# Two attention layers on one core: gate products moved to the end of the second attention, context shift rows on another queue, one modulation one tile later

## The chip, the core and the metric

The kernel runs on one core of a Trainium2 chip. The metric is the device time of one execution in microseconds (us). The core has TensorE for matrix products (PE in the profile, with its weight loads as PEld), VectorE (DVE), ScalarE (ACT), GpSimd (POOL) and SyncE (SP), which here only issues transfers. Each engine works through its own instruction stream in order; an instruction that must wait for another engine or for a transfer holds up all that stands behind it on its engine.

## What is computed

Two layers over 1024 latent tokens and 256 context tokens of width 1024, all in float32. Each layer modulates a normed input, runs attention, gates the result and adds it to the stream:

```python
shift, scale, gate = adaln_params(c, w_mod, b_mod)          # silu(cond) @ w_mod + b_mod, split in 3
shift_c, scale_c, gate_c = adaln_params(c_ctx, w_mod, b_mod)
h = rms_norm(x, norm_w) * (1.0 + scale[:, None, :]) + shift[:, None, :]
hc = rms_norm(ctx, norm_w) * (1.0 + scale_c) + shift_c
y, yc = mixer(h, hc, mixer_params, cos, sin, with_ctx_out)  # attention * silu(g), times w_out
x = x + gate[:, None, :] * y
```

Layer 0 is grouped-query attention (16 query heads, 4 key heads, 64 wide); latent tokens read context and latent keys, context tokens read context alone. Layer 1 is multi-head latent attention: keys and values come from a 256-wide compressed row through `w_kv_b`, queries from a 384-wide one. Layer 1 returns only the latent stream, so its context tokens give keys and values but no output, and only the gate of `c` (not of `c_ctx`) is needed there.

## The kernel before

**Stages, in order of time.** (1) Layer 0's modulation and projections up to about 300 us, by a hand-written plan. (2) Layer 0's attention, about 330 to 704 us. (3) Layer 0's output projection, 704 to 825 us, which also norms, modulates and transposes the tokens for layer 1. (4) The keys and values of layer 1 ("kv stage"), 825 to about 925 us. (5) Layer 1's queries and gate path, to 1140 us. (6) Layer 1's attention, 1140 to 1544 us. (7) Layer 1's output projection to the end.

**Precision.** Most matrix products are made in three parts (high times high, high times low, low times high) of values that are split in two: ACT casts the high half, DVE or POOL subtracts it (`split`, `load_weight`, `modulate`). Weights come through a ring of three raw buffers of [128, 1024] float32 (`rawp`, tag `wraw`), are cast on ACT (line 184) and subtracted on DVE or POOL (line 163).

**Attention.** `Attention.run` goes through units, one head of latent queries each (1024 queries, ten key tiles of 128) and, in layer 0, four more for the context queries of a key group (two key tiles). For each key tile TensorE makes five (layer 0: four) score products per half, ACT takes the exponential into `p` (line 607), and beside them TensorE makes the maxima of later units, which DVE reduces out of PSUM (lines 454, 465, 495, 497). After the last key tile `do_av` multiplies by the values (line 654). POOL adds the `p` tiles of a unit up (line 640). The order on PE, DVE, ACT and POOL is that of the program (`manual_schedule`); SP's order, and that of most other stages, is laid out by a scheduler when the kernel is built.

The row maxima are folded into the scores as an extra row, the shift row: `do_shift` turns the maxima on DVE (line 95, into `turned`) and copies two rows with a transfer into the unit's operand (`crow`): line 521, issued by ACT while `run` is under way. The turns run at one point of each unit, between its scores and its `do_av` (line 805); in the same place stand the sums of the unit before (`total_by_squares`), the transposing reductions of this unit (line 99, `squares`) and, on every second unit while some are left, the casts of an output weight piece (lines 818 to 821).

**Layer 1's gate.** Its gate vector is a product of `l1_w_mod` (transposed, rows 2048 to 3071) with a row `u`. `mod_cols` makes it as eight DVE instructions of 128x1024 with a sum (line 265), `mod_cols_end(2)` adds the bias, turns the result and stores it to `gated[1]`; it is read at the start of stage 7 (`load_x`, line 864). The eight stand in the kv stage, one per token tile, in the `later_with_cols` step of `staged`; each loads 512 KB into a `wraw` buffer. DVE's order in the kv stage is the program's (`in_order`), so each of them stands between the latent split of one tile and the key norm of another.

**Layer 0's output projection.** Each of ten token tiles takes 48 products (lines 120 to 122); `add` multiplies by the gate row, adds the old x (buffer `xt`, four of them), and `sink0` stores it to `x1d`, norms it in place (lines 305, 144, 146, 307) and gathers tiles in pairs. `modulate` transposes a pair on TensorE (line 319, 16 transposes), scales and shifts it on DVE (line 323) and splits it on ACT and DVE/POOL. `sink0` calls `flush(1)` at tiles 2, 4, 6 and 8, so that pair 0 (tiles 0 and 1) is modulated behind tile 2, pair 1 behind tile 4, and so on. The first two tiles are finished together, since the projection starts on partial sums.

## Time and profile before

| | |
|---|---|
| median of 3 runs | 1639.27 us (1636.88 to 1641.38) |
| profiled execution, its own time | 1638.23 us |
| its span, first to last instruction | 1636.3 us |
| mean granted TensorE clock | 0.995 |
| TensorE busy of the span | 98% |
| DVE, POOL, ACT busy | 70%, 59%, 39% |
| HBM moved | 171.23 MB read, 73.63 MB written |

The profile is one execution. "Busy" is the time in which an engine had an instruction; a wait is the idle time before an instruction, put down to what released it. In rows of a timeline the first number is the start in us from the first instruction, the second the duration in us; a row can stand for several like instructions ("x15"), and the idle time before it, with its releaser, is in brackets at the end. Rows of a wait view give the total in us, the number of times and the longest. "PEq", "ACTq" and "SPq" mark the sequencer of an engine, which issues transfers. Line numbers (L265) are those of the kernel before.

### The profile page before, as it was taken

To read this page: it belongs to the slowest core of one execution; us is meant where nothing else is said; L and a number is where in the kernel's file an instruction comes from. 1 tells how busy PE (TensorE), PEld (TensorE's weight loads), DVE (VectorE), ACT (ScalarE), POOL (GpSimd) and SP (SyncE) were. 2 spreads that over 40 slices of the span, in tenths; PEclk is the share of its full clock that TensorE was granted. 3 is DMA by queue.
4 is the path that set the end of the run, shared out by engine and by line. 5 is a ranking of instruction groups with operands and counts; after the bars stand their busy time and mean duration, and the time that the engine had idled before them with its cause. 6 is when DMAs were issued, how large, how long until landed. Compare 5 with 4: busy or idle time off the path is not lost.

```text
span 1636.3 us, 26486 instructions
## 1 busy us (share of the span) xinstructions
PE 1596.0 (98%) x9788; PEld 1178.3 (72%) x9788; DVE 1150.5 (70%) x1951; ACT 641.2 (39%) x943; POOL 961.7 (59%) x629
## 2 busy tenths in 40 slices
PE   7999999999999999999989999999999999999998
PEld 5776788865554555577878798987776767767587
DVE  2674876679998988746576767755778888788231
ACT  3652321235654555522244543341444544435310
POOL 2673640138999999923245555450768878777521
PEclk9999999999999999999999999999999999999999
DMA  8636566742533342274246867768456565562451
GB/s 285 213 106 192 170 196 231 215 134 56 130 82 98 94 108 78 71 224 152 96 138 182 239 200 201 221 202 197 114 137 154 124 149 117 136 145 70 131 179 64
DMA packets 215325, 246.77 MB, mean 151 GB/s; under 512 B 19802, under 2 KB 157266, under 8 KB 215196
## 3 DMA queue, kind: packets, MB, share of 16 engines
q1 hardware_dynamic: 214228, 244.83, 53.7%
q8 instruction: 77, 1.26, 0.3%
q14 instruction: 52, 0.43, 0.1%
q10 hardware_dynamic: 968, 0.25, 0.1%
HBM read 171.23 MB, written 73.63 MB: 150 GB/s over the span
## 4 chain that ended last, share of the span: by engine, by line
PE 84%; DMA 5%; DVE 4%; POOL 2%; ACT 2%; issue 2%; SPq 1%; DVEq 0%; POOLq 0%; ACTq 0%
PE st L600 21%; PE avt L654 9%; PE av L654 9%; PE mm L120 8%; PE mm L122 8%; PE mm L121 8%; PE mx L452 4%; PE y L120 3%; PE y L121 3%; PE y L122 3%; PE mx L486 2%; DVE wb L163 1%; DMA q1l<-tl 1%; PE mx L462 1%; DMA mraw<-in_l_w_mod 1%
## 5 line engine op out<-in xcount | busy, mean ns | idle before, releaser
L640 POOL TENSOR_TENSOR acp<-acp,p 128x1024 f32<-128x1024 f32 x188 | 448.6, 2386 | 12.6
L607 ACT ACTIVATE p<-st 128x1024 f32<-128x1024 f32 x328 | 336.3, 1027 | 154.5 <-PE st L600 145.7
L454 DVE TENSOR_REDUCE m<-mx 128x1 f32<-128x512 f32 x256 | 175.8, 691 | 66.2 <-PE mx L452 60.3
L640 POOL TENSOR_TENSOR acp<-p 128x1024 f32<-128x1024 f32 x34 | 81.5, 2398 | 191.7 <-ACT p L607 191.7
L495 DVE TENSOR_REDUCE m<-mx 128x1 f32<-128x1024 f32 x128 | 150.2, 1219 | 39.4 <-PE mx L486 38.9
L654 PE MATMUL avt<-p,v 128*64 128x512 f32 x672 | 149.3, 596 | 0.7 <-ACT p L607 0.6
L654 PE MATMUL av<-p,v 128*64 128x512 f32 x640 | 141.1, 595 | 0.0
L163 POOL TENSOR_TENSOR wb<-wraw,wa 128x512 fp32r<-128x512 f32 (+3 forms) x65 | 91.0, 1415 | 80.4 <-ACT wa L184 80.4
L120 PE MATMUL mm<-wa,hh 128*128 128x512 f32 (+2 forms) x336 | 126.1, 375 | 1.7 <-ACT hh L1041 1.1
L600 PE MATMUL st<-QH,KH 64*128 64x512 f32 x320 | 122.5, 407 | 0.6 <-DVE gth L354 0.5
L122 PE MATMUL mm<-wa,hl 128*128 128x512 f32 (+2 forms) x336 | 121.5, 362 | 1.6 <-DVE hl L1044 1.6
L121 PE MATMUL mm<-wb,hh 128*128 128x512 f32 (+2 forms) x336 | 121.1, 360 | 0.0
L600 PE MATMUL st<-QH,KL 64*128 64x512 f32 x320 | 117.9, 391 | 0.0
L600 PE MATMUL st<-QL,KH 64*128 64x512 f32 x320 | 117.6, 390 | 0.0
L654 PEld LDWEIGHTS avt<-p,v 128*64 128x64 f32 x672 | 46.0, 137 | 93.8 <-issue 82.9
L654 PEld LDWEIGHTS av<-p,v 128*64 128x64 f32 x640 | 44.3, 137 | 87.9 <-issue 87.3
L120 PE MATMUL mm<-hh,wa 128*128 128x512 f32 (+1 forms) x264 | 103.0, 390 | 0.9 <-ACT th L102 0.9
L120 PE MATMUL y<-wa,oh 128*128 128x512 f32 (+1 forms) x268 | 103.3, 386 | 0.0
L122 PE MATMUL y<-wa,ol 128*128 128x512 f32 (+1 forms) x268 | 102.8, 384 | 0.0
L121 PE MATMUL y<-wb,oh 128*128 128x512 f32 (+1 forms) x268 | 102.8, 384 | 0.0
L122 PE MATMUL mm<-hh,wb 128*128 128x512 f32 (+1 forms) x264 | 101.3, 384 | 0.0
L121 PE MATMUL mm<-hl,wa 128*128 128x512 f32 (+1 forms) x264 | 101.3, 384 | 0.0
(267 smaller groups left out, 4045.1 us busy)
## 6 DMA issues: line engine op xcount, KB each, us to landing
wraw<-in_l_w_in SPq DMA_DIRECT2D x28, 512.0 KB
wcols<-in_l_w_mod_t SPq DMA_DIRECT2D x24, 512.0 KB
KH<-k1h SPq DMA_DIRECT2D x32, 320.0 KB
KL<-k1l SPq DMA_DIRECT2D x32, 320.0 KB
rb<-rrow SPq DMA_DIRECT2D x72, 128.0 KB
mraw<-in_l_w_mod SPq DMA_DIRECT2D x16, 512.0 KB
wraw<-in_l_w_out SPq DMA_DIRECT2D x16, 512.0 KB
QA<-q0h SPq DMA_DIRECT2D x32, 256.0 KB
```

Source lines behind the costliest of these rows:

```text
L120: pe.matmul(ps, lhsT=lh(k), rhs=rh(k), start=first and i == 0, stop=False)
L121: pe.matmul(ps, lhsT=lh(k), rhs=rl(k), start=False, stop=False)
L122: pe.matmul(ps, lhsT=ll(k), rhs=rh(k), start=False, stop=last and i == len(ks) - 1)
L163: eng.tensor_sub(lo, a, b)
L452: pe.matmul(held["m"][:, cs], lhsT=q[:, t * P:(t + 1) * P], rhs=k[:, ks], start=j == 0, stop=j == len(pairs) - 1)
L454: dve.reduce_max(s["m"][:, i, n:n + 1], held["m"], axis=AX.X)
L486: pe.matmul(m[:, n * 512:n * 512 + 512], lhsT=q[:, i * P:(i + 1) * P], rhs=k[:, n * 512:n * 512 + 512], start=True, stop=True)
L495: dve.reduce_max(s["m"][:, i, 0:1], m, axis=AX.X)
L600: pe.matmul(ps[:, n * 512:(n + 1) * 512], lhsT=lh, rhs=rh, start=j == 0, stop=j == last)
L607: act.activation(p, ps, AF.Exp, scale=self.ops["scale"])
L640: pool.tensor_add(t, a, b)
L654: pe.matmul(s["av"][64 * n:64 * n + 64, :], lhsT=s["v"][:, kt, u["vc"]:u["vc"] + 64], rhs=p[:, n * 512:(n + 1) * 512], start=kt == kts[0], ...
```

## The change

Three things are edited.

1. The shift rows of context units are issued by SP while `run` is under way; those of latent units stay on ACT.
2. In `sink0`, `flush` is no longer called at tile 2 but at tile 3, before tile 3 joins tile 2 in the list of held pairs. Pair 0 is modulated behind the fourth tile (tile 3), pair 1 behind tile 4 as before.
3. The eight gate products of layer 1 and the load of `u` leave the kv stage. `run` gets a table `beside` of calls by unit and by whether the group is the unit's last; they run just ahead of `do_av`. In layer 1's attention unit 10 loads the first two weight pieces, units 11, 12 and 13 make one product each, unit 14 two, and the first group of unit 15 (the last unit, whose key tiles are cut in six and four) the last three and the end. Each product but the last two loads the piece two further on.

```diff
@@ Attention.__init__
+            self.beside = {}
@@ do_shift, turn
-                    (act if self.running else sp).dma_start(raw(s["crow"][n]), r[4 * n:4 * n + 4, :])
+                    (act if self.running and u["kind"] == "lat" else sp).dma_start(raw(s["crow"][n]), r[4 * n:4 * n + 4, :])
@@ Attention.run
                             self.squares(u, p2s[n1 // 2:])
+                        self.beside.get((t, int(end)), lambda: None)()
                         if t % 2 and end:
@@ sink0
-            if tt % 2 == 0:
+            if tt % 2 == 0 and tt != 2 or tt == 3:
                 flush(1)
-            else:
+            if tt % 2:
                 hold.append((tt // 2, xs_of[tt // 2]))
@@ kv stage
-        u = st.enter_context(tc.tile_pool(name="urow1", bufs=1, **right)).tile([P, D], F32, name="u0", tag="u0")
-        sp.dma_start(u, ud[0:1, :].broadcast_to([P, D]))
-
-        def gate_cols(k):
-            w = rawp.tile([P, D], F32, name="wcols", tag="wraw")
-            sp.dma_start(w, ins["l1_w_mod_t"][2 * D + k * P:2 * D + (k + 1) * P, :])
-            mod_cols(w, u.unsqueeze(1), w, 2, k, (0,))
-            if k == KT - 1:
-                mod_cols_end(2)
...
-            staged(range(TT), kv_compress, kv_latent, later_with_cols, later, kv_expand, store_all_but_last)
+            staged(range(TT), kv_compress, kv_latent, later, later, kv_expand, store_all_but_last)
@@ ahead of layer 1's at.run
+    u = stE.enter_context(tc.tile_pool(name="urow1", bufs=1, **right)).tile([P, D], F32, name="u0", tag="u0")
+    sp.dma_start(u, ud[0:1, :].broadcast_to([P, D]))
+    cols = {}
+
+    def gate_fetch(k):
+        cols[k] = rawp.tile([P, D], F32, name="wcols", tag="wraw")
+        sp.dma_start(cols[k], ins["l1_w_mod_t"][2 * D + k * P:2 * D + (k + 1) * P, :])
+
+    def gate_cols(n):
+        for _ in range(n):
+            k = cols.pop("next", 0)
+            mod_cols(cols[k], u.unsqueeze(1), cols[k], 2, k, (0,))
+            cols["next"] = k + 1
+            if k + 2 < KT:
+                gate_fetch(k + 2)
+            if k == KT - 1:
+                mod_cols_end(2)
+
+    at.beside = {(10, 1): lambda: [gate_fetch(k) for k in range(2)], (11, 1): lambda: gate_cols(1), (12, 1): lambda: gate_cols(1),
+                 (13, 1): lambda: gate_cols(1), (14, 1): lambda: gate_cols(2), (15, 0): lambda: gate_cols(3)}
     at.run(24, 2, pieces, lambda: first.extend(fetch_first(1, 3)))
```

## The prediction

> **What bounds the kernel now.** The page's first section comes first:

> ```profile
> span 1636.3 us, 26486 instructions
> PE 1596.0 (98%) x9788; PEld 1178.3 (72%) x9788; DVE 1150.5 (70%) x1951; ACT 641.2 (39%) x943; POOL 961.7 (59%) x629
> ```

> TensorE lacks 40.3 us of the span. The change takes no product from it, so it can win only where TensorE stands still or runs at a lower clock. So I read the waits of PE next (us in total, times, longest):

> ```profile
> PE mmk L120 <- DVE kn L1714: 2.3, 2, 1.5
> PE tp L319 <- DVE xt L307: 2.2, 1, 2.2
> PE tp L1955 <- DVE tl L103: 2.0, 1, 2.0
> PE mx L486 <- DVE m L495: 1.9, 2, 1.4
> ...
> PE st L600 <- ACT os L675: 1.1, 1, 1.1
> ...
> PE mmv L120 <- ACT v L1736: 1.0, 1, 1.0
> ...
> PE mmv L120 <- ACT sq L1729: 0.8, 1, 0.8
> ```

> Each of the three edits has its own waits here: L1714, L1736 and L1729 in the kv stage (mmk, mmv), L319 at pair 0, L486 and L600 in layer 0's attention. I then read the timelines around each.

> **Edit 3, what it removes.** First the steady part of the kv stage, one tile long, by the windows view (length, then busy us of PE, PEld, DVE, ACT, POOL, clock):

> ```profile
> 877.66:887.49 9.83, 9.83 (x61) 8.77 (x60) 6.74 (x17) 4.50 (x13) 5.98 (x8) 1.00 0.70 202
> ```

> PE is busy for all of it, so a shorter DVE gains nothing here. What can go are the waits at the ends. The products, and the stretch in which the last one stands (DVE, then POOL, then ACT):

> ```profile
> L265 DVE SCALAR_TENSOR_TENSOR wcols<-wcols,u x8: 1201/1204/1843, 850.6 to 907.5; 128x1024 f32<-128x1024 f32 x8
> 907.53 1.84 DVE L265 SCALAR_TENSOR_TENSOR wcols<-wcols,u 128x1024 f32<-128x1024 f32 x1
> 909.77 0.15 DVE L271 TENSOR_TENSOR top<-cols,colsT 128x8 f32<-128x8 f32 x1
> 909.96 0.86 DVE L95 STREAM_TRANSPOSE turned<-top 32x32 f32<-32x32 f32 x4
> 910.85 0.69 DVE L1731 TENSOR_REDUCE kss<-sq 128x8 f32<-128x512 f32 x1
> 905.91 2.38 POOL L163 TENSOR_TENSOR wb<-wraw,wa 128x384 fp32r<-128x384 f32 x2
> 910.91 0.51 ACT L184 CAST wa<-wraw 128x384 fp32r<-128x384 f32 x1 [2.30 <-DMA wraw<-in_l_w_in]
> ```

> Ahead of the key sums at 910.85 stand 1.84 + 0.15 + 0.86 = 2.85 us that go. They delay L1714, for which PE waits 2.3 us in two places. ACT waits 2.30 us for a weight piece whose buffer comes from the ring that the products' loads also use; without them it loads sooner, and the copy of v behind it, for which PE waits 1.0 us, too. So the drain's 3.3 us go nearly whole; I take 2.9, since the two POOL roots per tile stay in DVE's chain. At the fill, the 0.8 us at 863.9 stands behind three products (850.65, 854.77, 859.27) and goes. The other waits before 858 come ahead of the first product or from ACT, and stay. Sum: **3.7 us**, bounds 1.0 (only the buffer wait) and 4.1 (all of these waits). The eight loads, the load of u and the store to gated leave SP here too.

> **Edit 3, what it adds.** At the attention's end, one unit's gap and the last unit's rows:

> ```profile
> 1400.00:1500.00 100.00, 100.00 (x742) 69.91 (x742) 81.73 (x135) 42.67 (x44) 75.61 (x36) 1.00 0.51 120
> 1441.19 2.31 DVE L99 TRANSPOSE_TENSOR_REDUCE squares<-p 128x64 f32<-128x2048 f32 x1
> 1445.66 1.39 DVE L454 TENSOR_REDUCE m<-mx 128x1 f32<-128x512 f32 x2 [2.16 <-PE mx L452]
> 1439.03 4.80 POOL L640 TENSOR_TENSOR acp<-acp,p 128x1024 f32<-128x1024 f32 x2
> 1528.86 9.72 POOL L640 TENSOR_TENSOR acp<-acp,p 128x1024 f32<-128x1024 f32 x4
> 1540.35 3.77 DVE L871 TENSOR_TENSOR ol<-oraw,oh 128x896 fp32r<-128x896 f32 x3 [16.54 <-ACT oh L870]
> 1532.04 1.75 SPq L839 DMA_DIRECT2D oraw<-od  x3
> 1541.94 0.64 PE L720 MATMUL mx<-acp,twos 128*32 128x256 f32 x8
> ```

> In units 11 to 13 the product stands where DVE now idles 2.16 us. It needs 1.20 to 1.84 us (the second beside POOL's subtractions), so it fits: 0. In unit 14 no maxima follow that PE waits for. In unit 15 DVE idles 16.54 us and the three products need 3.6 to 5.5, but POOL adds without pause beside them. If each holds an addition back by its own 1.2 us, the last addition ends at 1538.6 + 3.6 = 1542.2 against PE's 1541.94: 0.3 us lost. Bounds 0 and 3.6. I take **0.3**. On SP the three oraw loads now wait for the last products' buffers, and behind them sg, od, gb and xt; with products that end by 1537 the loads come about 4 us later than 1532, while ol starts at 1540 and PE has three tiles to make: 0, and 2 if that cover is gone. The moved 4.7 MB fall on 100 us with a DMA share of 0.51: 0.

> [...]

> **Edit 2, pair 0.** PE, DVE, the chain and two windows:

> ```profile
> 737.34 0.30 PE L319 MATMUL tp<-ident,xt 128*128 128x128 f32 x1 [0.29 <-DVE x_ms L144]
> 739.80 2.81 PE L319 MATMUL tp<-ident,xt 128*128 128x128 f32 x15 [2.16 <-DVE xt L307]
> 738.44 1.30 DVE L307 TENSOR_SCALAR xt<-xt,x_rs 128x1024 f32<-128x1024 f32 x1 [0.58 <-DMA x1d<-xt]
> 735.46 2.88 DMA x1d<-xt
> 737.05:740.50 3.45, 1.00 (x7) 0.84 (x8) 2.82 (x6) 0.85 (x1) 1.82 (x2) 1.00 0.73 213
> 740.50:743.90 3.40, 3.40 (x15) 3.11 (x14) 3.40 (x8) 2.18 (x4) 0.78 (x2) 0.50 0.09 22
> ```

> The norm in place waits for the store of the same tile, and the transposes wait for the norm: 0.29 + 2.16 = 2.45 us idle. Right behind it the clock is 0.50 for 3.40 us, all of them busy: 1.70 us more. One tile later (about 11 us) the tile has been ready since 739.7, so both go: **4.15 us**, bounds 2.45 (the clock drops elsewhere) and 4.15. What is late next: pair 1's second tile has about 12 us from its last product to its transposes, where pair 0's had the same and lost 2.45 with two tiles finished at once; here one is. The loads of x for tiles 4 and 5 need pair 0's buffers and start some 7 us later; with 2.88 us a tile (the store's row) they land before tile 4's addition, 11 us on. SP's stores and oraw loads may queue behind these; I cost that 0, its price is the 2 us of another norm.

> [...]

> **Edit 1, shift rows.** ACT, DVE, then the same place one context unit later, then the tile's own view:

> ```profile
> 495.83 0.58 ACTq L521 DMA_DIRECT2D shift<-turned  x1
> 496.98 2.38 ACTq L521 DMA_DIRECT2D shift_ctx<-turned  x2
> 499.40 1.14 ACT L184 CAST wa<-wraw 128x512 fp32r<-128x512 f32 x2 [8.68 <-DMA sg<-sgd]
> 495.85 2.31 DVE L99 TRANSPOSE_TENSOR_REDUCE squares<-p 128x64 f32<-128x2048 f32 x1
> 500.57 1.86 DVE L163 TENSOR_TENSOR wb<-wraw,wa 128x512 fp32r<-128x512 f32 x1 [2.41 <-ACT wa L184]
> 529.88 0.50 PE L486 MATMUL mx<-KA,QA 64*128 64x512 f32 x2 [0.57 <-DVE m L495]
> L600 PE MATMUL st<-shift_ctx,minus x16: 385/388/394, 431.7 to 699.9; 64*128 64x512 f32 x16
> L521 ACTq DMA_DIRECT2D shift_ctx<-turned x8: 580/580/619, 405.3 to 669.9; - x8
> ```

> Of the four context turns only this one is followed by a wait: 1.1 (os) and 1.4 (m, of the 1.9) = 2.4 us. Without the two issues ACT casts at 496.4 instead of 499.4, DVE subtracts when its reduction ends (495.85 + 2.31 = 498.2) instead of 500.57, and the maxima follow 2.4 us sooner. One unit on, with the casts in time, 0.57 remain, so I take 2.4 - 0.4 = **2.0 us**, bounds 0 (the latent row still waits behind SP, and the casts with it) and 2.4. On SP the row waits for DVE's turn, with QA, QL and rb queued behind; the first use (431.7) is 26 us behind the first issue (405.3), so that is 0, at worst 2.

> **Sum.** 3.7 + 4.15 + 2.0 - 0.3 = 9.55. On the profiled execution: 1638.23 - 9.55 = 1628.7; it lies 1.04 under the median, so for the median 1639.27 - 9.55 = **1629.7 us**.

> **Rivals.**
> A. DVE's and POOL's own chain keeps the kv stage's end: edit 3 wins 1.0 or less, 1632.4, and with its 2 us of tail 1634.1. For it: POOL's roots stay; against: 2.85 us leave the chain at its latest point. 0.15.
> B. Pair 0 behind tile 3 meets another wait of 2 us and the low clock: edit 2 wins nothing, 1633.9. For it: x loads later; against: 11 us of room. 0.10.
> C. More goes than that: the 2.0 us at L1955 lies in a stage whose order the scheduler lays out anew, and weight pieces now load sooner; with 1.7 for a low clock behind it as at pair 0, 3.7 less: 1626.0. 0.12.
> D. Slower: the same new order sets casts and subtractions of weight pieces between the query tiles, so that PE stalls there as at L1955, 3.7 us each. From the third on it outweighs the gain: 1629.7 + 3 x 3.7 = 1640.8, from the fourth 1644.5. For it: one such stall stands there already; against: only one in some 200 us. 0.08.
> E. The edits don't bite: the scheduler leaves the waits in new places, 1638 to 1640. 0.05.

> **How the numbers follow.** The forecast (1627.5 to 1632) has 0.50. About 0.3% (4.9 us) is what a measurement here can tell from no change: 1634.4 and 1644.2. Faster: 0.50 + 0.13 of A + 0.05 of B + 0.12 = 0.80, of which I keep 0.77 for the part of the forecast lost to several small shortfalls. Slower: 0.04 of D and 0.01. Same: the rest, 0.18. The range leaves out D, E and the far end of C: 1625.0 to 1637.5.

> **What would show it.** No PE wait on L307 and a clock of 1.00 around pair 0; no wait on L675 near 501; waits on L1714, L1736 and L1729 under 1 us in sum; the products at 1.2 to 3.6 us in units 11 to 15 with no PE wait on DVE maxima, and under 1 us at L720. It is wrong if PE's idle time falls by less than 5 us, or if new waits appear in the query stage or at layer 1's output projection.

## The result, and the profile after

| | before | changed |
|---|---|---|
| median, 4 runs each on one chip | 1638.30 us (1636.88 to 1641.38) | 1622.22 us (1620.82 to 1623.37) |
| ratio | | 0.9899, 95% interval 0.9883 to 0.9914 |
| profiled execution, its span | 1636.3 us | 1620.2 us |

The change wins 16.1 us, by the interval 14.1 to 19.2. Forecast were 9.55 us, with 1625.0 as the lower end of the range: the direction was right, the size too small. One run of a kernel below (edit 3 alone) took 3203.56 us at a granted clock of 1.00, for a reason that the record does not show; its ratio leaves that run out. The first lines of the page of the changed kernel, and its waits of PE (us in total, times, longest); its line numbers are one or two higher, and in the query stage 13 lower:

```profile
span 1620.2 us, 26475 instructions
PE 1590.2 (98%) x9788; PEld 1182.7 (73%) x9788; DVE 1159.2 (72%) x1951; ACT 641.4 (40%) x943; POOL 961.1 (59%) x629
...
PE tp L1703 <- DVE kvn L1684: 3.7, 3, 1.3
...
PE tp L1942 <- DVE tl L103: 2.3, 2, 2.0
PE mx L487 <- DVE m L496: 1.8, 2, 1.2
PE y L108 <- ACT oh L872: 1.6, 2, 1.0
...
PE mmv L120 <- ACT v L1738: 0.5, 1, 0.5
```

PE's waits on L319, L675 (os) and L1714 are gone from the list, and of the fill's waits on `v` and `sq` nothing is left. But PE's idle time (span less busy) falls only from 40.3 to 30.0 us, 10.3; the other 5.8 us lie in PE's busy time, though it makes the same 9788 products. That PE is busy for fewer microseconds over the same work is the first thing to explain here.

To place the gain, take the same matrix product in both traces (the n-th with the same operands) and subtract its starts. The gain up to a stage's first product and up to its last one differ by what the stage won:

| place | won, us | forecast |
|---|---|---|
| start, to layer 0's attention (code unchanged) | 1.1 | 0 |
| layer 0's attention ahead of the turn, near 466 | -0.3 | 0 |
| turn near 496 (edit 1) | 1.5 | 2.0 |
| pair 0 (edit 2) | 4.5 | 4.15 |
| kv stage (edit 3) | 7.8 | 3.7 |
| query stage | 3.6 | 0 |
| layer 1's attention | -1.2 | 0 |
| its end and the output projection | -1.05 | -0.3 |

The sum, before rounding, is 16.1. Two rows of the table make most of the surplus: the kv stage and the query stage.

### The profile page after: what moved, and what is told of

It reads as the page before. It is cut to its first block, busy times and chain, and to the rows that moved or that the text cites. A ratio compares the mean times of both kernels' runs of the same rounds, so it can differ in the third digit from the quotient of the medians.

```text
span 1620.2 us, 26475 instructions
## 1 busy us (share of the span) xinstructions
PE 1590.2 (98%) x9788; PEld 1182.7 (73%) x9788; DVE 1159.2 (72%) x1951; ACT 641.4 (40%) x943; POOL 961.1 (59%) x629
## 3 DMA queue, kind: packets, MB, share of 16 engines
q8 instruction: 77, 1.26, 0.3%
## 4 chain that ended last, share of the span: by engine, by line
PE 87%; DVE 5%; DMA 3%; POOL 2%; ACT 1%; issue 1%; SPq 0%; DVEq 0%; ACTq 0%; POOLq 0%
PE st L601 19%; PE mm L120 9%; PE avt L655 8%; PE mm L122 8%; PE mm L121 8%; PE av L655 8%; PE mx L453 4%; PE y L121 4%; PE y L122 4%; PE y L120 4%; PE mx L487 2%; PE mx L463 1%; DVE wb L163 1%; DVE wcols L265 1%; DMA mraw<-in_l_w_mod 1%
## 5 line engine op out<-in xcount | busy, mean ns | idle before, releaser
L163 POOL TENSOR_TENSOR wb<-wraw,wa 128x512 fp32r<-128x512 f32 (+3 forms) x65 | 92.0, 1431 | 75.4 <-ACT wa L184 75.4
L120 PE MATMUL mm<-wa,hh 128*128 128x512 f32 (+2 forms) x336 | 125.6, 374 | 1.1 <-ACT hh L1043 1.1
L120 PE MATMUL mm<-hh,wa 128*128 128x512 f32 (+1 forms) x264 | 103.1, 390 | 0.0
L120 PE MATMUL y<-wa,oh 128*128 128x512 f32 (+1 forms) x268 | 102.9, 384 | 0.0
```

Source lines behind the costliest of these rows:

```text
L120: pe.matmul(ps, lhsT=lh(k), rhs=rh(k), start=first and i == 0, stop=False)
L163: eng.tensor_sub(lo, a, b)
```

## The experiments

All times are device times, each against runs of the kernel before on the same chip (medians 1636.99 to 1637.44). "Ledger" is the comparison above, with the first profile of before as the reference, at one place of one profiled execution.

**The three edits, each alone.** Each kernel is the one before with one of the diff's three parts.

> The kernel before with edit 1 alone (context shift rows by SP). Theory A, that each edit's share is what the changed kernel's PE timeline shows at its own place: 1.2 us less than before (the wait for os, 1.08, goes; of the wait for m 1.2 stays, since the DVE subtraction is longer beside POOL), and nothing in the kv and query stages. Theory B, that the surplus over the forecast (about 6 us) comes from the scheduler's new order whichever edit is made: 3 us or more less here, with waits gone in the query stage too.

> The kernel before with edit 2 alone (pair 0 modulated behind tile 3). Theory A: PE's waits at L319 (0.29 and 2.16) go, and so does a clock of 0.50 right behind them where a run of before has it: 2.7 to 4.5 us less. No other stage changes. Theory B: also less in the kv stage, whose first tiles follow 90 us on.

> The kernel before with edit 3 alone (gate products at the attention's end). Theory A: the kv stage wins 7.8 us (3.8 at its first tiles, 4.0 at its last), the query stage 0.9 to 1.9 by waits that go (the one at tl L103 of 2.0 stays; a clock of 0.50 behind it comes or not), the end loses 1.0: in sum 8 to 11 us less. Theory B, as forecast: 3.4 us less from the edit itself, the rest only together with the other edits.

| | median, us | ratio, interval | gain by the ratio |
|---|---|---|---|
| edit 1 | 1636.38 | 0.9997, 0.9988 to 1.0006 | 0.5 (-1.0 to 2.0) |
| edit 2 | 1632.50 | 0.9965, 0.9951 to 0.9978 | 5.7 (3.6 to 8.0) |
| edit 3 | 1630.24 | 0.9951, 0.9937 to 0.9964 | 8.0 (5.9 to 10.3) |

The three sum to 14.2, near the 16.1: the edits add up, and a surplus that comes whichever edit is made (theory B) is not seen. By the ledger edit 1 alone wins 1.7 at its turn, edit 2 alone 4.5 at pair 0 and nothing in the kv stage (5.0 before it, 5.1 behind it), edit 3 alone 7.9 in the kv stage. Edit 1's gain is too small for its timing to tell. It also has a price that nobody forecast: in all six profiles with this edit PE loses 0.26 to 0.30 us near 466, and in none without it; what makes it stays open. So edit 1 wins 1.2 to 1.5 us in sum.

Why edit 1 wins less than 2.4: the timelines at that turn, DVE and POOL with edit 1 alone, then POOL of before (DVE's subtraction there: 500.57, 1.86 us):

```profile
493.74 2.31 DVE L99 TRANSPOSE_TENSOR_REDUCE squares<-p 128x64 f32<-128x2048 f32 x1
495.98 2.68 DVE L163 TENSOR_TENSOR wb<-wraw,wa 128x512 fp32r<-128x512 f32 x1
495.73 2.38 POOL L640 TENSOR_TENSOR acp<-acp,p 128x1024 f32<-128x1024 f32 x1
```

```profile
497.05 4.83 POOL L640 TENSOR_TENSOR acp<-acp,p 128x1024 f32<-128x1024 f32 x2
```

The subtraction follows the reduction at once, as forecast, but lasts 2.68 us (2.81 in the changed kernel) where it had lasted 1.86. In both kernels it ends 0.55 us after the POOL addition that was running when it began: 498.66 after 498.11, and 502.43 after 501.88. It begins earlier and waits longer, so 0.8 to 0.95 us of the gain are given back, and a wait for m of 1.1 to 1.2 stays.

**Is ACT still the bound at that turn?** All shift rows on SP, the latent ones too:

```diff
-                    (act if self.running else sp).dma_start(raw(s["crow"][n]), r[4 * n:4 * n + 4, :])
+                    sp.dma_start(raw(s["crow"][n]), r[4 * n:4 * n + 4, :])
```

> The kernel before with all shift rows issued by SP, latent ones too. If the ACT casts of the weight piece were still the bound at the turn near 496, the wait for m (1.0 to 1.2 us with edit 1 alone) shrinks by up to 1 us. If DVE's own reduction and subtraction are the bound there, as the changed kernel's trace says, nothing is won against edit 1 alone. A loss comes if the latent rows stand behind SP's waits and scores wait for their shift row: then waits at st by st<-shift in every unit, 16 units of 0.5 us or more.

1656.50 us, ratio 1.0113 (1.0097 to 1.0128): 18.5 us slower. PE's waits in layer 0's attention, and SP ahead of the first of them:

```profile
PE st L600 <- DMA shift<-turned: 12.0, 2, 6.2
PE mx L486 <- DVE m L495: 1.6, 2, 1.0
```

```profile
478.69 0.38 SPq L744 DMA_DIRECT2D od<-os  x1
479.11 0.48 SPq L734 DMA_DIRECT2D sg<-sgd  x1
479.64 0.59 SPq L1415 DMA_DIRECT2D QA<-q0h  x1
480.34 1.38 SPq L521 DMA_DIRECT2D shift<-turned  x2
```

The wait for m is as with edit 1 alone (1.6 us in sum in both), so the ACT casts are no longer the bound there. The loss came in two units, not in all sixteen as the expectation had it: a latent row that stands behind SP's od, sg and QA makes PE wait 5.8 and 6.2 us. Each wait brings 6.83 us at a clock of 0.50 with it, so that by the ledger the two cost 8.2 and 8.6 us. That the changed kernel leaves these rows on ACT is what makes edit 1 safe.

**The kv stage: DVE's time, or the ring?** The kernel before with short products (all, then only those with k < 4), and with whole products but no loads:

```diff
-            mod_cols(w, u.unsqueeze(1), w, 2, k, (0,))
+            mod_cols(w[:, :8], u.unsqueeze(1)[:, :, :8], w[:, :8], 2, k, (0,))
```

```diff
-            w = rawp.tile([P, D], F32, name="wcols", tag="wraw")
-            sp.dma_start(w, ins["l1_w_mod_t"][2 * D + k * P:2 * D + (k + 1) * P, :])
-            mod_cols(w, u.unsqueeze(1), w, 2, k, (0,))
+            dve.scalar_tensor_tensor(u, u, 0.5, u, op0=ALU.mult, op1=ALU.add, accum_out=sums_of[2][:, k, 0:1])
```

> The kernel before with the eight gate products of the kv stage made over 8 of 1024 columns; the loads, their ring buffers and SP's stream stay. It leaves out 1016 of 1024 columns of each gate product. Theory A, that DVE's time in the kv stage's chain makes the loss: the kv stage wins 6 to 7.5 us of the 7.8, at its first tiles 3.5 to 3.8. Theory R, that the ring's buffers and loads make it: 2 us or less, all at the end, and the first tiles keep their waits at L1702 (1.37) and on v L1736 (0.68 twice).

> The same, but only the first four products over 8 columns, the last four whole. It leaves out 1016 of 1024 columns of four gate products. Theory A: the kv stage wins the 3.8 us of its first tiles and nothing at its end, where the waits at L1714 (1.47, 0.80) and L1736 (0.99) stay. Rival, that a delay at the first tiles is what reaches the end: 6 us or more.

> The kernel before with the eight products made on the resident row tile, with no loads and no ring buffers; DVE's instructions have the same size. It leaves out the weight matrix of the gate products (another sum is formed). Theory A: the first tiles keep all their waits (3.8 us); at the end ACT's wait for wraw (2.30) goes and of the 4.0 us there at most 1 to 1.5 is won. Theory R: 2 us or more at the end and something at the first tiles.

| | median, ratio | fill, ledger | end, ledger |
|---|---|---|---|
| all short | 1627.37, 0.9947 (0.9932 to 0.9963) | 3.6 | 2.5 |
| first four short | 1630.73, 0.9960 (0.9945 to 0.9975) | 3.6 | 1.0 |
| no loads | 1638.78, 1.0007 (0.9995 to 1.0018) | 0.0 | 0.0 |
| changed kernel | | 3.8 | 4.0 |

(Without loads the fill has the same four waits as before: 1.36, 0.67, 0.68 and 0.76 us. A slot of half clock, of which more below, fell into it in that profile and took 1.4 us; it is left out of the 0.0.) The fill's gain comes with DVE's shorter work alone. At the end each cause hides behind the other: free of the loads alone nothing is won, free of DVE's work alone 2.5, free of both 4.0. (With the first four short, 1.0 was won at the end where the expectation had nothing: the wait for v fell there from 1.0 to 0.2.) With short products the end's wait is this one of ACT, on the load, with the copy of v behind it:

```profile
910.20 0.51 ACT L184 CAST wa<-wraw 128x384 fp32r<-128x384 f32 x1 [3.26 <-DMA wraw<-in_l_w_in]
910.62 0.58 ACT L1736 COPY v<-mmv 128x512 f32<-128x512 f32 x1
```

A rival is left open here. The order of PE's and ACT's instructions in this stage is laid out when the kernel is built, and it is not the same in these kernels. With short products and in every kernel with edit 3, three of PE's transposes in the fill and ten of ACT's instructions stand earlier than before; without loads PE's order is the old one, and so are the fill's waits. So the runs show that DVE's work is the cause, but not how much of the fill's gain comes from waiting less in the same order and how much from the new order. In the query stage, up to 1140 us, PE, DVE and ACT have the same order before and after.

**How a product of 1.20 us makes a wait of 1.37.** The fill of the kernel before, POOL, DVE and PE, then the changed kernel's POOL at the same tile:

```profile
850.23 0.26 POOL L1693 TENSOR_TENSOR krt<-kvn,ropeB 128x32 f32<-128x32 f32 x1
850.56 1.41 POOL L1694 TENSOR_TENSOR kvn<-krt,krt 128x32 f32<-128x32 f32 x1
850.65 1.20 DVE L265 SCALAR_TENSOR_TENSOR wcols<-wcols,u 128x1024 f32<-128x1024 f32 x1
851.79 0.14 DVE L1677 TENSOR_SCALAR kvms<-kvss 128x1 f32<-128x1 f32 x1
852.02 0.28 PE L1702 MATMUL tp<-ident,kvn 128*32 128x128 f32 x1 [1.37 <-POOL kvn L1694]
853.91 0.50 PE L120 MATMUL mmk<-wa,kvh 128*128 128x512 f32 x1 [0.68 <-ACT v L1736]
857.98 0.40 PE L120 MATMUL mm<-wa,hh 128*128 128x288 f32 x1 [0.68 <-ACT v L1736]
```

```profile
843.64 0.25 POOL L1696 TENSOR_TENSOR kvn<-krt,krt 128x32 f32<-128x32 f32 x1
```

POOL's small addition took 1.41 instead of 0.25 us: it ends 0.12 us behind DVE's product. And DVE's next norm (L1677) starts 1.1 us late. To tell the two apart the product is replaced by an instruction that reads one input:

```diff
-            mod_cols(w, u.unsqueeze(1), w, 2, k, (0,))
+            dve.tensor_scalar(w, w, 0.5, 0.0, op0=ALU.mult, op1=ALU.add, accum_out=sums_of[2][:, k, 0:1])
```

> The kernel before with each gate product replaced by a DVE instruction over the same 128x1024 tile that reads one input instead of two. It leaves out the factor u of the gate products. Theory L, that the first wait of the kv stage's fill (1.37 at L1702) comes from POOL being held beside DVE's two-input instruction (its addition L1694 took 1.41 us instead of 0.25): that addition takes 0.25 to 0.4 us and the wait at L1702 falls to some 0.2. Theory C, that DVE's own time is enough: at an unchanged duration of 1.2 us on DVE the wait stays at 1.0 or more. If the instruction itself takes half the time the run says less: then the later waits on v L1736 (0.68 twice) shrink by about as much.

1633.26 us, ratio 0.9978 (0.9967 to 0.9989). The first such instruction, POOL ahead of it, and PE's wait:

```profile
847.68 0.25 POOL L1694 TENSOR_TENSOR kvn<-krt,krt 128x32 f32<-128x32 f32 x1
847.77 1.20 DVE L1767 TENSOR_SCALAR_CACHE_REDUCE wcols<-wcols 128x1024 f32<-128x1024 f32 x1
847.99 0.28 PE L1702 MATMUL tp<-ident,kvn 128*32 128x128 f32 x1 [0.21 <-POOL kvn L1694]
```

DVE works for the same 1.20 us, POOL's addition takes 0.25 us again, and the wait at L1702 falls from 1.37 to 0.21; by the ledger the fill wins 1.3 of its 3.8 us. Theory L holds for that wait. The other 2.5 stay where DVE's own time stays; that they pass through DVE's late norm is argued, not shown.

**The end: SP.** The changed kernel with a table of calls that begins and ends one unit earlier:

```diff
-    at.beside = {(10, 1): lambda: [gate_fetch(k) for k in range(2)], (11, 1): lambda: gate_cols(1), (12, 1): lambda: gate_cols(1),
-                 (13, 1): lambda: gate_cols(1), (14, 1): lambda: gate_cols(2), (15, 0): lambda: gate_cols(3)}
+    at.beside = {(10, 1): lambda: [gate_fetch(0), gate_fetch(1), gate_cols(1)], (11, 1): lambda: gate_cols(1), (12, 1): lambda: gate_cols(1),
+                 (13, 1): lambda: gate_cols(2), (14, 1): lambda: gate_cols(3)}
```

> The changed kernel with the products earlier: one in each of units 10 to 12, two in 13, three in 14, none in 15. Theory A, that the 0.98 us wait at the first product of the output projection comes from SP, where the three oraw loads stand behind the gate store that waits for the last products: that wait goes, 1.0 us less than the changed kernel (about 1621 against 1622). Rival: the second product of unit 13 does not fit DVE's gap of 2.16 us and PE waits there for maxima, some 1 us, so that nothing is won or 0.5 lost.

> The changed kernel with the products in units 10 to 14, again, on the same chip as the changed kernel itself. If the end's wait behind SP's gate store is what it wins: 1.1 to 1.4 us under the changed kernel, sometimes 1.7 more where a slot of half clock would have followed that wait (as in the run of edit 3 alone). If it was a luckier chip: the two agree within 0.5 us.

> The changed kernel, beside the one with the earlier products. The first product of the output projection waits 1.0 to 1.3 us for oh, the 2.0 us at tl L103 stay, and a slot of half clock follows them only if they lie whole between two edges of the raster of 3.413 us.

Earlier products: 1618.63 us (0.9884, 0.9871 to 0.9897), and on another chip 1619.37 (1617.86 to 1620.72; 0.9891, 0.9877 to 0.9906) beside the changed kernel's 1623.22 (1620.91 to 1623.28; 0.9911, 0.9894 to 0.9927). The ranges of the single runs don't overlap there, though the intervals of the ratios do. The medians lie 3.85 us apart there, more than the 1.1 to 1.4 expected. By the ledger of the two profiles, 4.4 us apart, 1.6 lie at the end; 2.6 lie in the query stage, where only the changed kernel's profile has a slot of half clock. SP of the changed kernel (first profile) and the projection's first product, then SP of the earlier products (second run):

```profile
1517.81 0.30 SPq L274 DMA_DIRECT2D gated<-turned  x1
1518.20 0.45 SPq L735 DMA_DIRECT2D sg<-sgd  x1
...
1520.67 2.09 SPq L737 DMA_DIRECT2D rb<-rrow  x2
1522.80 1.80 SPq L841 DMA_DIRECT2D oraw<-od  x3
1528.15 0.50 PE L108 MATMUL y<-wa,oh 128*128 128x512 f32 x1 [0.98 <-ACT oh L872]
```

```profile
1504.62 0.30 SPq L274 DMA_DIRECT2D gated<-turned  x1
...
1512.72 1.75 SPq L841 DMA_DIRECT2D oraw<-od  x3
```

In the changed kernel the loads start 5.0 us behind the gate store, about 8 us later in the program than before (1532.04 less the 17.1 us won by then is 1514.9). The first product of the projection (1528.15) then waits 0.98 us for oh; in the other profiles of the changed kernel 1.26 and 1.53, with edit 3 alone 2.0. With the earlier products no wait of PE is left from 1130 us to the end of layer 1's attention, in both runs. The rival, a wait for maxima in unit 13, did not show.

**The clock.** The changed kernel once more:

> The changed kernel again, for the clock: theory G, that the clock of 0.50 covers one slot of a fixed raster of about 3.41 us and follows a slot in which PE was busy under half, with a phase that differs from execution to execution: the waits of 2.0 us at tl L103 in the query stage is followed by a slot of 0.50 in those executions alone in which it lies whole in one slot (some 4 in 10). Rival: the clock depends on the wait's length alone, and since it did not fall behind this wait in the changed kernel's first profile it does not here. Otherwise as the first profile, 1622.

1620.85 us (0.9899, 0.9883 to 0.9916). The wait of 2.0 us at tl L103 in the query stage is in all fourteen profiles. Windows of the slot in which it begins and of the next one, in before, in the first profile of the changed kernel and in its third (length, busy us of PE, PEld, DVE, ACT, POOL, clock):

```profile
996.54:999.95 3.41, 1.38 (x11) 1.09 (x10) 2.97 (x9) 0.00 (x0) 1.46 (x3) 1.00 0.96 294
999.95:1003.36 3.41, 3.41 (x12) 3.41 (x11) 3.25 (x12) 1.84 (x4) 2.22 (x3) 0.50 1.10 360
```

```profile
979.87:983.28 3.41, 2.74 (x17) 2.38 (x15) 3.15 (x10) 0.49 (x1) 3.24 (x4) 1.00 0.87 224
983.28:986.69 3.41, 2.06 (x13) 2.09 (x14) 3.20 (x9) 0.82 (x2) 0.61 (x2) 1.00 1.11 372
```

```profile
979.95:983.36 3.41, 1.38 (x10) 1.05 (x9) 2.98 (x9) 0.00 (x0) 1.97 (x3) 1.00 0.92 258
983.36:986.77 3.41, 3.41 (x12) 3.41 (x13) 3.34 (x11) 1.72 (x4) 1.71 (x3) 0.50 1.11 366
```

The same wait is followed by half the clock in the first and third and not in the second, where an edge splits it: the raster of theory G holds, and its rival falls with the third profile. Its "busy under half" (1.71 us) is no exact bound: slots with 1.66 us busy (before, at 911.15) and 1.53 (earlier products, first run, at 979.96) were followed by the full clock, slots with 1.73 (edit 2 alone, at 496.44) and 2.14 (all rows on SP, at 1122.63) by half. Within every profile the starts of such slots lie whole multiples of 3.4133 us apart (before: 740.53 and 999.95, 76.0 of them). In five of the fourteen profiles the wait lay whole between two edges, and in these five alone the slot of 0.50 followed; in the other nine an edge cut it, at worst 1.88 on one side.

## Why the prediction came out too low

- **Edit 3, what it removes: the step that failed.** The forecast took 3.7 us, and the stage won 7.8. Two parts of the step were wrong. (a) "The other waits before 858 come ahead of the first product or from ACT, and stay": three of them, 1.37, 0.68 and 0.68 us at 852.02, 853.91 and 857.98, come behind the first product (850.65) or the second (854.77) and go when those are short. POOL's held addition makes the first; the two on v, with ACT as the last link, go with DVE's shorter work, through its late norm or through the order laid out for it. (b) Idle time was taken as the whole price of a wait: the change "can win only where TensorE stands still or runs at a lower clock". The windows of the stage, from the same product to the same product, before, changed, and with one-input instructions:

```profile
828.00:940.00 112.00, 100.84 (x578) 84.92 (x578) 77.20 (x184) 53.21 (x135) 56.28 (x65) 1.00 0.67 197
```

```profile
821.09:925.27 104.18, 98.74 (x578) 85.61 (x578) 66.95 (x163) 54.19 (x136) 52.26 (x65) 1.00 0.58 169
```

```profile
825.12:935.33 110.21, 101.33 (x578) 84.87 (x578) 75.75 (x184) 53.02 (x135) 51.63 (x65) 1.00 0.67 201
```

 All hold the same 578 products, at a clock of 1.00. In the changed kernel the stage is 7.82 us shorter, PE is idle for 5.72 us less, and busy for 2.10 us less. Around one wait it looks like this (kernel before, PE):

```profile
921.59 0.39 PE L122 MATMUL mmv<-wa,kvl 128*128 128x512 f32 x1
922.78 0.50 PE L120 MATMUL mmk<-wa,kvh 128*128 128x512 f32 x1 [0.80 <-DVE kn L1714]
923.11 0.39 PE L121 MATMUL mmk<-wb,kvh 128*128 128x512 f32 x1
923.35 0.40 PE L122 MATMUL mmk<-wa,kvl 128*128 128x512 f32 x1
```

 Such products otherwise start 0.23 us apart, and a row's 0.39 overlaps the next one's. Here the starts are 1.19 and then 0.33 apart: 0.96 + 0.10 = 1.06 us are lost where the idle column says 0.80. Over the stage the price is 7.82/5.72 = 1.37 times the idle time, with short products 6.2/4.6 = 1.33. It is no fixed factor: with one-input instructions, where most waits became shorter or split but did not go, PE is idle for 2.28 us less and the stage only 1.79 us shorter. The 4.1 us that the step fell short are most of the 6.5 us by which the forecast did. Its own bounds, 1.0 to 4.1, excluded the result for the same two reasons.
- **Edit 3, what it adds.** In units 11 to 15 no wait of PE came from the products. The 0.3 us that the forecast took for unit 15 did not come either, by a narrow margin: POOL's last addition ended 2.8 us later against PE's work than before, at 1524.23, and PE's product that reads it started at 1524.80:

```profile
1513.52 10.71 POOL L641 TENSOR_TENSOR acp<-acp,p 128x1024 f32<-128x1024 f32 x4
1524.80 0.64 PE L721 MATMUL mx<-acp,twos 128*32 128x256 f32 x8
```

 The loss of 1.05 us came by the path that the step costed at 0: oraw "about 4 us later" came 8 us later, since the gate store and the loads behind it follow each other on SP. In unit 15 the products took 1.80, 2.29 and 2.28 us beside POOL's work, and the small sum behind them 2.21; together with the turn and the store the end was at 1517.8, some 9.4 us after 1508.41. The three products alone took 6.2 us (1508.41 to 1514.64): more than the 3.6 to 5.5 of the forecast's sum. No run shows the 1.2 us by which each product was to hold one addition, nor the 3.6 us that the forecast allows a single product: the eight took 1.33 to 3.38 us, and POOL lost its 2.8 us on L740 (2.26 us, before 1.30), L741 (2.13, before 1.28) and the four additions (10.71, before 9.72).
- **Edit 2** was right: the waits at L319 are gone in every profile that has the edit, no other came, and 4.5 us were won for 4.15. All six profiles with this edit won the same 4.5 there against the profile of before, which had the slot of half clock. That slot followed pair 0's wait in seven of the eight profiles without the edit; in the eighth the place was 1.4 us shorter than before, so that the wait alone cost 3.1, where the idle columns said 2.45. In four of the eight the place was 2.5 to 2.7 us longer than before: their first wait at L319 was 1.7 to 2.3 us instead of 0.29, and the half clock held for two slots. So the price that edit 2 removes varies from 3.1 to some 7.2 us, and the timing's 5.7 fits that. That 4.15 came so close to 4.5 owes something to the profile that was read.
- **Edit 1** was right in kind, 1.5 to 1.8 for 2.0 at its turn: the size was off by the subtraction's 0.8 to 0.95 us beside POOL, and the 0.3 lost near 466 was not foreseen.
- **Rival C** was half seen. The wait at tl L103 stayed; only its slot of half clock (1.6 us) was absent, by the position of the edges and not by the new order. Of the rest of the 3.6 us in the query stage, the waits of 0.9 (th), 0.4 (QH) and 0.5 (gth) of before are absent in the first changed profile; in its third one two like the first two, 0.96 (qt) and 0.72 (QH), are back. Only the 0.5 stays away in every profile with edit 3 (it is away with short products too), and by the ledger it is worth 1.0 us. So no more than about 1 us of that row's 3.6 belongs to the change.
- **The range** left out that a slot of half clock behind one of the long waits costs 1.4 to 1.7 us and comes or not by the position of its edges: apart from start and end, the profiles of all kernels but the one with every row on SP have none to two such stretches, of one slot or two. Start and attention vary from profile to profile too: the start's 1.1 varies from 0.0 to 4.5, and the attention's -1.2 is shared by all four profiles of one other chip (-1.0 to -1.3), among them kernels without the products in the attention, and by none of the eight on two further chips. What makes it, at equal clock and without idle time, stays open.

## What to carry to other kernels

A wait can cost PE more than the idle time beside it (1.06 us for 0.80 in the case above): compare the stage's length at equal work, not the idle column. Here waits that went cost about a third more than their idle time (7.82 us for 5.72); waits that only got shorter won less than theirs (1.79 for 2.28). Before calling a wait "from another engine", follow it back over every engine to the work that one means to move: here a filler of 1.2 us that reads two inputs delayed its own engine's next step by 1.1 us and held a POOL addition of 0.25 us for 1.41. And work moved to a stage's end must be ready before the queue behind its store is needed: one unit earlier cost nothing here and took away a wait of 1.0 to 1.5 us.
